# Rotary embedding on one core: tables first on the SP queue, three batch rows ahead, four tiles

## Chip, cores and metric

The kernel runs on one core of a Trainium2 chip. The metric is the device time of one execution in microseconds, as the median of several runs. The profile is one more execution, recorded by the hardware profiler.

## The reference

Each pair of neighbouring values along the last axis is rotated by an angle that depends on the position in the sequence; batch rows and heads share the tables.

```python
batch, seq_len, num_heads, head_dim = (8, 2048, 16, 64)      # x, float32
x_pairs = x.reshape(batch, seq_len, num_heads, head_dim // 2, 2)
x1 = x_pairs[..., 0]
x2 = x_pairs[..., 1]
# cos, sin: (2048, 32), broadcast over batch and heads
out1 = x1 * cos - x2 * sin
out2 = x1 * sin + x2 * cos
out = np.stack([out1, out2], axis=-1).reshape(batch, seq_len, num_heads, head_dim)
```

## The kernel before

A batch row of x is 2048 positions of 16 heads of 64 values. It is laid over 128 partitions, 16 positions each, so a row is a tile of 128 x 16384 values. In memory it is float32 (64 KB a partition); in the chip's SBUF it is bf16 (32 KB a partition). The transfers of the POOL queue, started by GpSimd, convert on the way in and on the way out.

For each batch row b, `load(b)` (L56) brings the row into a tile `xt`, `rotate` computes in place, and `store(b)` (L59) writes it out. The tiles come from a pool of `NX` = 5 buffers, so `load(5)` must wait until the store of row 0 has landed, and so on. `rotate` is three VectorE operations over the whole row: x times the sine table into a work tile `qt` (L74), x times the cosine table in place (L75), and the sum of x and `qt` with its pairs swapped (L80). The sine table `s_tab` has its second value of each pair negated, which makes the swap right.

Two pieces are handled apart. The first `HEAD` = 2 of row 0's 16 positions, the head, come as float32 over the SP queue (L84) and are cast by ScalarE into the tile (L91); `load(0, HEAD)` brings the other 14. The last `TAIL` = 4 positions of row 7, the tail, are cast by ScalarE to float32 (L118) and stored over the SP queue (L119), after a one-element copy (L117) which waits until the store of row 6 has landed. Head, `qt` and tail share one buffer of the pool `stage`.

The order is written out by hand (`tc.manual_schedule()`), and each queue takes its instructions in that order. SP: head, cosine table, sine table, and at the end the tail. POOL: the loads of rows 0 to 4, the store of row 0, a one-element copy into `mark` (L106) that reads the last loaded tile and so waits for the load of row 4, the store of row 1, and then load 5, store 2, load 6, store 3, load 7, stores 4 to 7. VectorE: the tables (L93 to L95), the head's rotation, the rest of row 0, and rows 1 to 7.

A transfer over 128 partitions is spread over the core's 16 DMA engines: 8 partitions, and so 8 packets, on each. The same 16 engines serve the SP and the POOL queue.

Of the kernel before, what the change touches and what calls it, by code (L numbers as in the profile page):

```python
# [2 lines left out]

# [4 lines left out]


@with_exitstack  # L10
def kernel(
    ctx: ExitStack,
    tc: tile.TileContext,
    x: bass.AP,
    cos: bass.AP,
    sin: bass.AP,
    out: bass.AP,
):
    nc = tc.nc
    fp32 = mybir.dt.float32  # L20
    bf16 = mybir.dt.bfloat16
    mult = mybir.AluOpType.mult
    add = mybir.AluOpType.add

    B, S, H, D = x.shape
    P = 128
    K = S // P
    KP = 16
    D2 = D // 2
    HD = H * D  # L30
    NX = 5
    HEAD = 2
    TAIL = 4


    x_t = x.rearrange("b (p k) h d -> b p k (h d)", p=P, k=K)
    out_t = out.rearrange("b (p k) h d -> b p k (h d)", p=P, k=K)
    cos_t = cos.rearrange("(p k) c -> p (k c)", p=P, k=K)
    sin_t = sin.rearrange("(p k) c -> p (k c)", p=P, k=K)

    consts = ctx.enter_context(tc.tile_pool(name="consts", bufs=1))
    xpool = ctx.enter_context(tc.tile_pool(name="xpool", bufs=NX))
    stage = ctx.enter_context(tc.tile_pool(name="stage", bufs=1))

    cos_sb = consts.tile([P, K * D2], fp32)
    sin_sb = consts.tile([P, K * D2], fp32)
    c_tab = consts.tile([P, K, D], bf16)
    s_tab = consts.tile([P, K, D], bf16)

    mark = consts.tile([1, 1], bf16)  # L50
    tiles = {}

    def load(b, k0=0):
        if b not in tiles:
            tiles[b] = xpool.tile([P, K, HD], bf16, name="xt")
        nc.gpsimd.dma_start(out=tiles[b][:, k0:], in_=x_t[b, :, k0:])  # L56

    def store(b, k1=K):
        nc.gpsimd.dma_start(out=out_t[b, :, :k1], in_=tiles[b][:, :k1])  # L59

    def rotate(b, k0, k1):
        nk = k1 - k0
        xp = tiles[b][:, k0:k1]
        qt = stage.tile([P, KP, HD], bf16, name="qt", tag="work")

        def rows(a):
            return a.rearrange("p k (h e) -> p k h e", h=H, e=D)

        def tab(a):
            return dataclasses.replace(  # L70
                a, offset=a.offset + k0 * D, ap=[a.ap[0], [D, nk], [0, H], [1, D]]
            )

        nc.vector.tensor_tensor(out=rows(qt[:, :nk]), in0=rows(xp), in1=tab(s_tab), op=mult)  # L74
        nc.vector.tensor_tensor(out=rows(xp), in0=rows(xp), in1=tab(c_tab), op=mult)  # L75
        q_swap = dataclasses.replace(
            qt, offset=qt.offset + 1, ap=[qt.ap[0], [2, nk * HD // 2], [-1, 2]]
        )
        x3 = xp.rearrange("p k (a j) -> p (k a) j", j=2)
        nc.vector.tensor_tensor(out=x3, in0=x3, in1=q_swap, op=add)  # L80

    with tc.manual_schedule():
        head = stage.tile([P, TAIL, HD], fp32, name="st", tag="work")
        nc.sync.dma_start(out=head[:, :HEAD], in_=x_t[0, :, :HEAD])  # L84
        nc.sync.dma_start(out=cos_sb, in_=cos_t)
        nc.sync.dma_start(out=sin_sb, in_=sin_t)
        load(0, HEAD)
        for b in range(1, NX):
            load(b)

        nc.scalar.copy(out=tiles[0][:, :HEAD], in_=head[:, :HEAD])  # L91
        s2 = s_tab.rearrange("p k (i j) -> p (k i) j", j=2)
        nc.vector.tensor_copy(out=s2[:, :, 0], in_=sin_sb)  # L93
        nc.vector.tensor_scalar_mul(s2[:, :, 1], sin_sb, -1.0)  # L94
        nc.vector.tensor_copy(  # L95
            out=c_tab.rearrange("p k (i j) -> p (k i) j", j=2),
            in_=cos_sb.to_broadcast([P, K * D2, 2]),
        )
        for b in range(B):
            if b == 0:  # L100
                rotate(b, 0, HEAD)
                rotate(b, HEAD, KP)
            else:
                rotate(b, 0, KP)
            if b == 1:
                nc.gpsimd.tensor_copy(out=mark, in_=tiles[NX - 1][:1, K - 1, :1])  # L106
            if b < B - 1:
                store(b)

            if b >= 1 and b - 1 + NX < B:  # L110
                load(b - 1 + NX)
        store(B - 1, K - TAIL)

        tail = stage.tile([P, TAIL, HD], fp32, name="st", tag="work")
        nc.scalar.copy(out=tiles[B - 2][:1, 0, :1], in_=tiles[B - 1][:1, K - 1, :1])  # L117
        nc.scalar.copy(out=tail, in_=tiles[B - 1][:, K - TAIL :])  # L118
        nc.sync.dma_start(out=out_t[B - 1, :, K - TAIL :], in_=tail)  # L119


# [1 line left out]
_INS = ['x', 'cos', 'sin']  # L123
_OUTS = [((8, 2048, 16, 64), 'float32')]


# [23 lines left out]
```

## Time and profile before

The median of three runs is 317.25 us (317.14 to 317.61). The profiled execution has a span of 315.5 us from the first to the last instruction.

| What | Number |
|---|---|
| Median of three runs | 317.25 us |
| Span of the profiled execution | 315.5 us |
| VectorE, a whole row, one operation (L74, L75, L80; 7 of each) | 8.69 us |
| VectorE, row 0 without its head, one operation | 7.62 us |
| VectorE, the head, one operation | 1.22 to 1.23 us |
| VectorE, three table operations L93, L94, L95 | 0.45, 0.44, 0.68 us |
| ScalarE, cast of the head (L91) and of the tail (L118) | 1.90 and 3.60 us |
| GpSimd, copy into `mark` (L106), at 102.11 us | 2.93 us |
| A transfer's issue on POOL | 0.53 to 0.67 us |
| A transfer's issue on SP | 0.35 to 0.43 us |
| Head, cosine, sine: issue to landing | 4.7, 13.4, 31.7 us |
| Load of row 0 without its head: issue to landing | 22.3 us |

The events around the queue, from the timeline in order of time (start, length, engine, line, operation, out and in, how many, and in brackets the idle time before and what ended it):

```profile
0.74 0.36 SPq L84 DMA_DIRECT2D st<-in_x_dram  x1
1.16 0.42 SPq L85 DMA_DIRECT2D cos_sb<-in_cos_dram  x1
1.24 2.80 POOL L56 DMA_DIRECT2D xt<-in_x_dram  x5 [0.80 <-PEq L145]
1.63 0.42 SPq L86 DMA_DIRECT2D sin_sb<-in_sin_dram  x1
...
61.93 0.54 POOL L59 DMA_DIRECT2D out_dram<-xt  x1 [57.89 <-DVE xt L80]
...
263.75 0.53 POOL L59 DMA_DIRECT2D out_dram<-xt  x1 [38.06 <-DVE xt L80]
295.36 0.19 ACT L117 COPY xt<-xt 1x1 bf16<-1x1 bf16 x1 [288.01 <-DMA out_dram<-xt]
295.46 3.60 ACT L118 CAST st<-xt 128x4096 f32<-128x4096 bf16 x1
299.08 0.35 SPq L119 DMA_DIRECT2D out_dram<-st  x1
```

A transfer's line shows when it was put into its queue, not when its data moved. Between the two lies the time that it stands behind earlier transfers: the store of row 0 was issued at 61.93 us, the last one at 263.75 us, 50 us before the end.

### The profile page before, as it was taken

The page shows a single profiled execution, that of the slowest core. Times are in us where ns is not written, and L with a number is a line of the kernel's source. Part 1 is how long each engine was busy: PE and PEld are TensorE (multiplying, and loading weights), DVE is VectorE, ACT ScalarE, POOL GpSimd, SP SyncE. Part 2 cuts the span into 40 slices and gives each one's busy share as a digit, 9 for nine tenths or more (in the row PEclk, how much of TensorE's full clock was granted, in tenths as well). Part 3 has the DMA queues.
Part 4 walks back from the last instruction along what each step waited for, and adds up shares of the span by engine and source line. Part 5 has one row for each costly group of instructions (what it writes and reads, how often), then busy time and mean ns, then how long its engine had stood idle before and what let it go on. Part 6 is the DMA issues. An engine that isn't in the chain of part 4 may idle for free.

```text
span 315.5 us, 125 instructions
## 1 busy us (share of the span) xinstructions
DVE 210.3 (67%) x30; ACT 6.9 (2%) x4; POOL 11.7 (4%) x21
## 2 busy tenths in 40 slices
DVE  0000799999999999999999993899509994000000
ACT  4000000000000000000000000000000000000400
POOL 3000000000000301010000100000000000000000
DMA  9899999999999999999999999999999999999997
GB/s 279 184 261 206 199 220 245 199 199 253 212 199 266 399 449 482 399 332 245 220 399 399 399 199 199 399 532 266 199 241 490 399 399 490 440 399 399 432 432 332
DMA packets 2880, 101.71 MB, mean 322 GB/s; under 512 B 320, under 2 KB 320, under 8 KB 576
## 3 DMA queue, kind: packets, MB, share of 16 engines
q0 software_dynamic: 2304, 98.04, 97.1%
q1 hardware_dynamic: 576, 3.67, 3.0%
HBM read 67.63 MB, written 67.11 MB: 427 GB/s over the span
## 4 chain that ended last, share of the span: by engine, by line
another core or an unknown queue 91%; DMA 1%; ACTq 1%; ACT 1%; issue 0%
DMA st<-in_x_dram 1%; ACTq L145 1%; ACT xt L91 1%; ACT xt L117 0%; ACTq L117 0%
## 5 line engine op out<-in xcount | busy, mean ns | idle before, releaser
L74 DVE TENSOR_TENSOR qt<-xt,s_tab 128x16384 bf16<-128x16384 bf16 (+2 forms) x9 | 69.7, 7743 | 19.1 <-DMA xt<-in_x_dram 18.8
L75 DVE TENSOR_TENSOR xt<-xt,c_tab 128x16384 bf16<-128x16384 bf16 (+2 forms) x9 | 69.7, 7743 | 0.4
L80 DVE TENSOR_TENSOR xt<-xt,qt 128x16384 bf16<-128x16384 bf16 (+2 forms) x9 | 69.7, 7744 | 0.3
L93 DVE CAST s_tab<-sin_sb 128x512 bf16<-128x512 f32 x1 | 0.5, 453 | 33.4 <-DMA sin_sb<-in_sin_dram 33.4
L59 POOL DMA_DIRECT2D out_dram<-xt x8 | 4.3, 534 | 139.9 <-DVE xt L80 139.9
L56 POOL DMA_DIRECT2D xt<-in_x_dram x8 | 4.4, 560 | 72.8 <-DMA out_dram<-xt 72.0
L117 ACT COPY xt<-xt 1x1 bf16<-1x1 bf16 x1 | 0.2, 192 | 288.0 <-DMA out_dram<-xt 288.0
L106 POOL COPY mark<-xt 1x1 bf16<-1x1 bf16 x1 | 2.9, 2929 | 39.6 <-DMA xt<-in_x_dram 39.6
L118 ACT CAST st<-xt 128x4096 f32<-128x4096 bf16 x1 | 3.6, 3598 | 0.0
L91 ACT CAST xt<-st 128x2048 bf16<-128x2048 f32 x1 | 1.9, 1897 | 3.4 <-DMA st<-in_x_dram 3.4
L91 ACT ACT_TABLE_LOAD x1 | 1.3, 1283 | 0.7 <-PEq L134 0.7
L95 DVE CAST c_tab<-cos_sb 128x1024 bf16<-128x1024 f32 x1 | 0.7, 683 | 0.0
L94 DVE TENSOR_SCALAR s_tab<-sin_sb 128x512 bf16<-128x512 f32 x1 | 0.4, 444 | 0.0
L134 POOL MEMSET const-float32-0.0<- 128x1 f32 x1 | 0.1, 100 | 0.2 <-issue 0.2
L134 POOL MEMSET const-bfloat16-1.0<- 128x1 bf16 x1 | 0.1, 102 | 0.0
L134 POOL MEMSET const-float32-1.0<- 128x1 f32 x1 | 0.1, 100 | 0.0
L134 POOL MEMSET const-uint8-127<- 128x1 uint8 x1 | 0.1, 100 | 0.0
## 6 DMA issues: line engine op xcount, KB each, us to landing
xt<-in_x_dram POOLq DMA_DIRECT2D x7, 4096.0 KB, 57.6
out_dram<-xt POOLq DMA_DIRECT2D x1, 6144.0 KB, 47.8
xt<-in_x_dram POOLq DMA_DIRECT2D x1, 3584.0 KB, 22.3
out_dram<-st SPq DMA_DIRECT2D x1, 2048.0 KB, 15.5
st<-in_x_dram SPq DMA_DIRECT2D x1, 1024.0 KB, 4.7
cos_sb<-in_cos_dram SPq DMA_DIRECT2D x1, 256.0 KB, 13.4
sin_sb<-in_sin_dram SPq DMA_DIRECT2D x1, 256.0 KB, 31.7
out_dram<-xt POOLq DMA_DIRECT2D x7, 70.1
```

Of the source, the lines that this page charges most:

```text
L56: nc.gpsimd.dma_start(out=tiles[b][:, k0:], in_=x_t[b, :, k0:])
L59: nc.gpsimd.dma_start(out=out_t[b, :, :k1], in_=tiles[b][:, :k1])
L74: nc.vector.tensor_tensor(out=rows(qt[:, :nk]), in0=rows(xp), in1=tab(s_tab), op=mult)
L75: nc.vector.tensor_tensor(out=rows(xp), in0=rows(xp), in1=tab(c_tab), op=mult)
L80: nc.vector.tensor_tensor(out=x3, in0=x3, in1=q_swap, op=add)
L91: nc.scalar.copy(out=tiles[0][:, :HEAD], in_=head[:, :HEAD])
L93: nc.vector.tensor_copy(out=s2[:, :, 0], in_=sin_sb)
L94: nc.vector.tensor_scalar_mul(s2[:, :, 1], sin_sb, -1.0)
L95: nc.vector.tensor_copy(out=c_tab.rearrange("p k (i j) -> p (k i) j", j=2), in_=cos_sb.to_broadcast([P, K * D2, 2]),)
L106: nc.gpsimd.tensor_copy(out=mark, in_=tiles[NX - 1][:1, K - 1, :1])
L118: nc.scalar.copy(out=tail, in_=tiles[B - 1][:, K - TAIL :])
L145: with _tile.TileContext(nc) as tc:
```

## The change

On SP the order becomes sine table, cosine table, head. The pool of row tiles has four buffers instead of five, and three loads instead of five are issued ahead of the first store. After that a store and a load alternate: store 0, load 3, store 1, load 4, and so on to load 7, then stores 5 to 7. The copy into `mark` is gone. ScalarE's cast of the head stands after the table operations in the text; it is on an engine of its own, so its place there changes nothing in the order of any engine. The bytes, the operations on the rows and the tail are as they were.

```diff
-    NX = 5
+    NX = 4
+    AHEAD = 3
...
-    mark = consts.tile([1, 1], bf16)
...
         head = stage.tile([P, TAIL, HD], fp32, name="st", tag="work")
+        nc.sync.dma_start(out=sin_sb, in_=sin_t)
+        nc.sync.dma_start(out=cos_sb, in_=cos_t)
         nc.sync.dma_start(out=head[:, :HEAD], in_=x_t[0, :, :HEAD])
-        nc.sync.dma_start(out=cos_sb, in_=cos_t)
-        nc.sync.dma_start(out=sin_sb, in_=sin_t)
         load(0, HEAD)
-        for b in range(1, NX):
+        for b in range(1, AHEAD):
             load(b)
-        nc.scalar.copy(out=tiles[0][:, :HEAD], in_=head[:, :HEAD])
...
+        nc.scalar.copy(out=tiles[0][:, :HEAD], in_=head[:, :HEAD])
         for b in range(B):
...
-            if b == 1:
-                nc.gpsimd.tensor_copy(out=mark, in_=tiles[NX - 1][:1, K - 1, :1])
             if b < B - 1:
                 store(b)
-
-            if b >= 1 and b - 1 + NX < B:
-                load(b - 1 + NX)
+            if b + AHEAD < B:
+                load(b + AHEAD)
         store(B - 1, K - TAIL)
```

## The prediction

> **What bounds the kernel now.** I read the page's head and its 40 slices first: who is busy at the end, and who all the time?
>
> ```profile
> span 315.5 us, 125 instructions
> DVE 210.3 (67%) x30; ACT 6.9 (2%) x4; POOL 11.7 (4%) x21
> DVE  0000799999999999999999993899509994000000
> DMA  9899999999999999999999999999999999999997
> q0 software_dynamic: 2304, 98.04, 97.1%
> HBM read 67.63 MB, written 67.11 MB: 427 GB/s over the span
> ```
>
> VectorE has a third of the span free, at both ends. The sixteen DMA engines have nothing free. Next the windows (length, then DVE, ACT and POOL busy, clock, DMA share, GB/s), one inside a load, one inside a store:
>
> ```profile
> 60.00:70.00 10.00, 9.96 (x2) 0.00 (x0) 0.54 (x1) 1.00 0.98 210
> 110.00:120.00 10.00, 9.97 (x2) 0.00 (x0) 0.00 (x0) 1.00 0.98 419
> ```
>
> GB/s counts what is written: a load reads f32 and writes bf16, so 210 there and 419 in a store are the same rate on the f32 side. Then I went to the trace's single packet records. Call Lb and Sb the load and store of batch row b (L0 without its head, S7 without its tail). Each whole transfer is eight packets on every engine, 2.43 us each in a load and 2.45 in a store, packed back to back. The first packets of the POOL queue's sixteen transfers start at:
>
> ```
> L0 5.11  L1 22.73  L2 42.25  L3 61.57  L4 80.94  S0 101.26  S1 120.57  L5 139.89
> S2 159.21  L6 178.53  S3 197.85  L7 217.17  S4 236.49  S5 255.81  S6 275.12  S7 294.44
> ```
>
> From L2 on the spacing is 19.31 to 19.32 us in either direction, except 20.32 for L4. There the last packet of every engine, at 98.0 to 98.4, took 2.99 to 3.54 us instead of 2.43: some 0.95 us that I can't explain. The tail store's packets, from 305.27, share the engines with S7's and end at 314.26. No engine pauses from its first packet (1.75 us in the earliest) to its last. So the time is 1.75 + 312.5 of packets + 1.2 to close = 315.5 us, and the median of the runs, 317.25, has 1.75 more around it.
>
> The waits show what the DMA stream hides:
>
> ```profile
> POOL xt L56 <- DMA out_dram<-xt: 72.0, 3, 37.6
> DVE s_tab L93 <- DMA sin_sb<-in_sin_dram: 33.4, 1, 33.4
> DVE qt L74 <- DMA xt<-in_x_dram: 18.8, 2, 12.4
> ```
>
> VectorE stands 33.4 us at the start for the sine table, the third transfer on SP. That looks like the thing to win, but its last operation ends at 263.5, and 51 us of stores are still queued.
>
> **The change part by part.** What can move the time is bytes, packet cost, or an engine left without a packet. The bytes stay. So each part is asked: does it leave the queue dry?
>
> *SP order.* In the records of before, once POOL's packets arrive at 5.11, each engine takes one SP packet and one POOL packet in turn; the sine table needed a turn of about 2.2 us for each of its eight packets and its completion. Now the tables' 16 packets an engine run first, at 0.084 us: 1.34 us. The head's packets are 0.309 us. Before, the earliest engine needed 2.87 us for eight of them against 2.47, so a cold start costs about 0.4. By 5.11 an engine has served (5.11 - 1.75 - 1.34 - 0.4) / 0.309 = 5 head packets. Three and the completion remain, each in a turn of 2.13 + 0.31 = 2.44: the head lands at 5.11 + 4 x 2.44 = 14.9. If POOL's packets came sooner (three issues instead of five in 2.80 us), at most all eight take turns: 5.11 + 9 x 2.44 = 27.1. The low end is 5.6, with none left.
>
> Packet cost: 144 of 256 table packets took 96 ns between POOL's instead of 84, nine an engine, 0.11 us saved. For head packets in turns the nearest rows are the tail's: 644 against 611 ns, with their neighbour at 1828 instead of 1847: +0.014 each, +0.04 for three. Sum -0.07 us; with the cold start at 0 to 0.8 instead of 0.4, -0.5 to +0.5. I take -0.1.
>
> *VectorE's start.* The head's cast (1.90) runs to 16.9, three operations of 1.23 to 20.7. L0 lands at 1.24 + 22.3 = 23.5, so the head is hidden. L0's three operations of 7.62 end at 46.5, and S0 is issued 0.6 later (as 61.36 to 61.93 before) at 47.1.
>
> *Queue order, three loads ahead, four tiles.* The queue becomes L0 L1 L2 S0 L3 S1 L4 S2 L5 S3 L6 S4 L7 S5 S6 S7: the same sixteen pieces in the same sixteen slots, since a load and a store take equally long. A whole row costs VectorE 3 x 8.73 = 26.2 us. A transfer lands about 0.45 us after its last packet, which ends 0.45 after the next slot opens; the next issue follows. Working through:
>
> ```
>       ready because                      issued   slot opens   spare
> S0    row 0 done 46.5                      47.1        61.6     14.5
> L3    fourth tile, new: no wait            47.6        80.9     33
> S1    row 1 done 72.7                      73.2       101.3     28
> L4    waits for S0 to land 81.8            81.9       120.6     39
> S2    row 2 done 98.9                      99.5       139.9     40
> L5    waits for S1 to land 121.5          121.7       159.2     37
> S3    row 3: L3 lands 102, done 128.2     128.7       178.5     50
> L6    waits for S2 to land 160            160.2       197.9     38
> S4    row 4: L4 lands 140.7, done 166.9   167.4       217.2     50
> L7    waits for S3 to land 198.7          198.9       236.5     38
> S5    row 5: L5 lands 179.3, done 205.5   206         255.8     50
> S6    row 6: L6 lands 218, done 244.2     244.7       275.1     30
> S7    row 7: L7 lands 256.6, done 282.8   283.4       294.4     11
> ```
>
> The waits of L4 to L7 have the stores S2 to S5 queued behind them on POOL. Each wait ends (81.8, 121.5, 160, 198.7) before its store's row is done (98.9, 128.2, 166.9, 205.5), so none delays a store. The copy into `mark` (2.93 us on POOL at 102.11) goes; it stood ahead of S1, due at 120.57 anyway. Nothing is saved. The tail still waits for S6 and shares with S7: unchanged.
>
> *From issue to first packet.* Only one row shows it unhidden: L0, issued at 1.24, first packet 5.11, 3.9 us, VectorE idle. An upper bound with VectorE busy is S1: issued 104.98, running at 120.57, 15.6 us, most of it surely queueing. I take 3.9, the unhidden one. S0 then has 14.5 - 3.9 = 10.6 us to spare and S7 11 - 3.9 = 7.1. With 15.6 instead, S0 would be 1.1 us late; S7's issue finds VectorE idle, so L0's row fits it.
>
> The Trainium skill speaks against this margin. "SBUF — State Buffer", Who interferes with whom, says that GpSimd can't write descriptors while VectorE runs in a mode that holds the port pair they share, and adds that two-input operations hold only the read side. The trace has a GpSimd instruction held up: the copy at L106 took 2.93 us and ended at 105.04, with VectorE's operation that ended at 105.00. It reads SBUF, so it fits the milder reading. By the severe one S0 would wait for an operation's end, at most 8.7 us, and still be in time at 55.8; by the milder one the sum stays as it is.
>
> *Sum:* 315.5 - 0.1 = 315.4; with 1.75 around it 317.2 (317.15).
>
> **Rivals.**
>
> *A. Dry before S0 (slower).* Its place is slot 61.6. If the head takes all its turns (27.1), the cast ends at 29.0, the head's operations at 32.9, L0's at 55.8, and S0 is issued at 56.4. With 3.9 it is in time at 60.3; with one VectorE operation's length, 8.69, it comes at 65.1, 3.5 us late: 320.7. It decides once issue plus preparation passes 61.6. Bounds: 1.1 late (on-time head, 15.6) to 10.4 (late head, 15.6), 318.3 to 327.6. For it: no other slot comes so early in VectorE's work. Against: two long delays must coincide. Chance 0.12.
>
> *B. A price on each turn from load to store (slower).* The 0.95 us sit exactly ahead of the first store. Before had four such turns, now six. If each paid, 5 x 0.95 more: 321.9. Against: the other three turns (at 159.21, 197.85, 236.49) show 19.32 and nothing else. Chance 0.06.
>
> *C. The 0.95 us vanish (faster).* If they belong to five loads in a row, or to S0 standing alone in the queue until 104.98, the new order drops them: 316.2. If they belong to the first write of the output, or to chance, they stay. One event can't tell. Chance 0.14.
>
> *D. VectorE's chain counts after all (faster).* Rows start at 16.9 instead of 34.66: -17.8, 299.4. Against: the full DMA row and the 51 us after VectorE's end. Chance 0.02.
>
> **How the numbers follow.** The forecast, no change, 317.2, has 0.66. A measurement of this kernel can tell some 0.2%, 0.6 us, from no change. Faster is C and D, 0.16; same 0.66; slower is A and B, 0.18. The range runs from 316.1, just under C, to 319.0, which takes in the start-up's +0.5 and A's mild end, and leaves out D, B and most of A.
>
> **What would show it.** Right: packets back to back from 1.8 to 314 us, sixteen transfers 19.32 apart; sine waited for until about 4 us instead of 33.4; head landing near 15; S0 issued near 47; VectorE waiting for loads from row 3 on; S7 issued near 283. Wrong: a gap between L2's last packet and S0's first (A); last packets of 3 us before several stores (B); none anywhere (C); or a spacing other than 19.32 in the mixed stretch, which no part of my sum allows for.

## The result, and the profile after

The changed kernel took 319.73 us in the median of six runs (317.41 to 320.98), the kernel before 317.24 (317.14 to 317.61): a ratio of 1.0068, 95% interval 1.0052 to 1.0084. It is slower by 0.7%, and its runs spread over 3.6 us where those of before spread over 0.5. The forecast of no change was wrong, and 319.73 lies above the range. (Three single runs of later variants, near 328 us, stand in the medians below and are left out of the ratios.)

The page of the changed kernel, the lines that answer to those of before:

```profile
span 317.9 us, 125 instructions
DVE  1004999999999999709993199912999039980000
DMA  7999999999999999999999999999999999999994
HBM read 67.63 MB, written 67.11 MB: 424 GB/s over the span
```

Bytes are the same and the DMA row is as full as before in its middle. The new digits are at the ends: 7 instead of 9 in the first slice, 4 instead of 7 in the last. The waits and the first and last store of rows on POOL, from its waits and its timeline:

```profile
DVE s_tab L92 <- DMA sin_sb<-in_sin_dram: 3.5, 1, 3.5
ACT xt L98 <- DMA st<-in_x_dram: 23.9, 1, 23.9
DVE qt L74 <- DMA xt<-in_x_dram: 47.6, 4, 12.5
DVE qt L74 <- ACT xt L98: 23.0, 1, 23.0
...
55.12 0.54 POOL L59 DMA_DIRECT2D out_dram<-xt  x1 [52.15 <-DVE xt L80]
...
285.56 0.53 POOL L59 DMA_DIRECT2D out_dram<-xt  x1 [38.10 <-DVE xt L80]
```

The sine table came at once, as meant, and VectorE's 33.4 us wait for it fell to 3.5. But the head, now third on SP, came at 25.9 us, and VectorE waited 23.0 us for its cast instead (ACT xt L98). The first store was still issued 6.5 us before its slot at 61.6.

So where are the 2.4 us of span? In the windows at the end (length, DVE, ACT and POOL busy, clock, DMA share, GB/s), the kernel before is silent from 314.4 us on:

```profile
314.40:315.00 0.60, 0.00 (x0) 0.00 (x0) 0.00 (x0) 1.00 0.00 0
315.00:316.00 1.00, 0.00 (x0) 0.00 (x0) 0.00 (x0) 1.00 0.00 0
316.00:316.70 0.70, 0.00 (x0) 0.00 (x0) 0.00 (x0) 1.00 0.00 0
```

The changed one isn't:

```profile
314.40:315.00 0.60, 0.00 (x0) 0.00 (x0) 0.00 (x0) 1.00 0.06 27
315.00:316.00 1.00, 0.00 (x0) 0.00 (x0) 0.00 (x0) 1.00 0.04 16
316.00:316.70 0.70, 0.00 (x0) 0.00 (x0) 0.00 (x0) 1.00 0.05 23
```

A share of 0.04 to 0.06 of sixteen engines is one engine at work. The packet records say the same. A record gives a packet's queue, start, length and size, but not its engine; which packets belong to one engine is inferred from one starting where another ends. The tail is complete on fifteen engines between 313.9 and 314.6 us, and on the sixteenth at 316.73. Every engine has an equal, fixed share of every transfer, so one that is behind can't hand its packets on; the kernel ends when it ends.

This engine can be followed back through the packet records. The others got their first POOL packet at 3.48 to 3.77 us, right behind the two tables. This one got it at 5.14: with 3.59 for the median, 1.55 us behind. In between no engine started a packet (DMA share 0.00):

```profile
3.80:5.10 1.30, 1.02 (x3) 0.00 (x0) 0.00 (x0) 1.00 0.00 0
```

Its first packet took 2.45 us instead of 2.13: 0.32 more. At the first store the last load packet of the others is some 1.2 us longer than usual; its own last two took 2.88 and 3.96 us, 1.97 more than two at 2.43: 0.75 more. 1.55 + 0.32 + 0.75 = 2.62, against 316.73 - 314.15 = 2.58 at the end. The sixteen landing times of each transfer agree: the last of them is 1.83 us behind the middle for the load of row 0, 2.58 for the load of row 2, and 2.51 to 2.59 for every whole transfer after it.

### The profile page after: what moved, and what is told of

It is laid out like the page before. It is cut to its first block, busy times and chain, and to the rows that moved or that the text cites. A ratio compares the mean times of both kernels' runs of the same rounds, so it can differ in the third digit from the quotient of the medians.

```text
span 317.9 us, 125 instructions
## 1 busy us (share of the span) xinstructions
DVE 210.5 (66%) x30; ACT 6.9 (2%) x4; POOL 8.9 (3%) x20
## 4 chain that ended last, share of the span: by engine, by line
another core or an unknown queue 85%; DMA 8%; ACTq 1%; ACT 1%; SPq 0%; issue 0%
DMA st<-in_x_dram 8%; ACTq L142 1%; ACT xt L98 1%; SPq L85 0%; SPq L84 0%; ACT xt L114 0%; ACTq L114 0%
## 5 line engine op out<-in xcount | busy, mean ns | idle before, releaser
L98 ACT CAST xt<-st 128x2048 bf16<-128x2048 f32 x1 | 1.9, 1898 | 23.9 <-DMA st<-in_x_dram 23.9
```

## The experiments

All times are medians; each kernel was timed beside runs of the kernel before on the same chip (317.61 for the first four, 317.38 for the next four, 317.64, 317.63 and 317.70 for the three pairs after that). The code shows what is changed; "..." stands for lines left out. The first four ask which part of the change does it, whether the late engine comes back, and what the lengthened packets are.

**SP's old order in the changed kernel.**

```diff
-        nc.sync.dma_start(out=sin_sb, in_=sin_t)
-        nc.sync.dma_start(out=cos_sb, in_=cos_t)
         nc.sync.dma_start(out=head[:, :HEAD], in_=x_t[0, :, :HEAD])
+        nc.sync.dma_start(out=cos_sb, in_=cos_t)
+        nc.sync.dma_start(out=sin_sb, in_=sin_t)
```

> The changed kernel with SP's old order (head, cosine, sine); three loads ahead, four tiles and the alternation stay. Theory 1 (start): in the changed kernel SP's table packets are used up by 3.7 us, the head's are not there yet, and an engine whose first POOL packet comes late (5.14 us instead of 3.5 to 3.8) stands idle and stays behind to the end; with the head first, SP's packets last beyond 5 us and cover it. It expects 317.2, spread under 0.6 us over the runs, all engines ending within 0.6 us of one another. Theory 2 (queue): the alternation of stores and loads, or the shorter batch of issues, makes one engine fall behind. It expects 319.7 as in the changed kernel, with one engine some 2 us behind the rest.

Measured: 317.34 (316.34 to 317.51), ratio 0.9987, interval 0.9979 to 0.9996. All engines ended between 314.17 and 314.33. Theory 2 falls: the queue plan alone costs nothing. No engine was late from the start: the load of row 0 landed on all sixteen between 23.15 and 23.57 us. This kernel also ran its queue dry, since with the sine last VectorE is late again. From its timeline:

```profile
61.33 8.69 DVE L74 TENSOR_TENSOR qt<-xt,s_tab 128x16384 bf16<-128x16384 bf16 x1
61.86 0.54 POOL L59 DMA_DIRECT2D out_dram<-xt  x1 [58.87 <-DVE xt L80]
```

The store was issued at 61.86, and its first packet ran at 62.97, 1.1 us later, while the VectorE operation of the first line still ran until 70.0. The engines had their last load packet through by 61.6 to 62.1, so they stood empty for 0.8 to 1.5 us. No load packet is lengthened here: the pause stands where the lengthening stood, and the store begins about when it does on fifteen engines of the changed kernel (62.97 to 63.13 here, 62.7 to 63.4 there). One of the eleven runs took 316.34, 1 us less than the rest; it has no trace.

**SP's new order alone, in the kernel before.** The two table lines go ahead of the head's as in the change; nothing else.

> The kernel before with SP's new order alone (sine, cosine, head); five loads ahead, five tiles, the copy into mark stay. Theory 1 (start): the engines run out of SP packets at 3.7 us here too, and with five issues in the first batch POOL's packets come no earlier than in the changed kernel: 318.6 to 321, spread over 1 us. Theory 2 (queue): 317.2, spread under 0.6 us.

Measured: 317.81 (317.20 to 319.78), ratio 1.0020, interval 1.0002 to 1.0037. A half miss: five of eleven runs are above 318.1, four of them above 318.6, but six show no loss. The SP order is needed for the loss, and something in the queue plan makes it frequent.

**The changed kernel again.** No edit.

> The changed kernel once more, unaltered, for a second profile and five more times. Theory 1 (start): some 319.5 with a spread of 1 to 3.5 us, and the engine that ends last is the one whose first POOL packet came last, by about the same amount plus what it loses at the first store. If instead the late engine is late from a later point (the first store, or the tail), theory 1 falls.

Measured: 319.66 (317.38 to 328.4; the 328.4 is a single run that no trace here explains). In its trace the latest first packet is at 5.49 us, 2.0 behind the median, and takes 3.02 instead of 2.13; the last engine ends at 317.09, 2.95 behind. The lateness is there at the start, as theory 1 says.

**A tiny store ahead of all others.**

```diff
         nc.sync.dma_start(out=sin_sb, in_=sin_t)
+        nc.sync.dma_start(out=out_t[0, :1, 0, :16], in_=cos_sb[:1, :16])
```

> The kernel before, with a store of 16 values of the cosine table into the first row of the output added on SP behind the three loads; the store of row 0 overwrites it. It asks what the some 0.95 us belong to by which the last load packets ahead of the first store are longer, in both kernels. If to the first write into the output, it moves to the tiny store near 15 us, and is partly hidden or not: last packets ahead of the first POOL store 2.43 us instead of 3.3, time 316.3 to 317.2. If to POOL's first turn from load to store, nothing changes: 317.2, last packets of 3.3 us at about 98 us.

Measured: 317.49 (317.34 to 317.61), ratio 0.9997, interval 0.9989 to 1.0006. The sixteen last load packets ahead of the first POOL store still took 3.01 to 3.28 us. So the lengthening does not belong to the first write into the output.

The next four ask whether it is cover that counts, whether the batch's length does, and again about the first store.

**The head second.**

```diff
         nc.sync.dma_start(out=sin_sb, in_=sin_t)
-        nc.sync.dma_start(out=cos_sb, in_=cos_t)
         nc.sync.dma_start(out=head[:, :HEAD], in_=x_t[0, :, :HEAD])
+        nc.sync.dma_start(out=cos_sb, in_=cos_t)
```

> The changed kernel with SP in the order sine, head, cosine. Theory 1 (start): what counts is that SP's packets keep every engine busy until its first POOL packet is there. Sine and head together are 0.67 + 2.47 us of packets from 1.9 us on, to about 5, with the cosine behind them: 317.2 to 317.5, spread under 0.8 us, while VectorE still gets the sine by 4 us. Rival (head's place): it is the tables being first that hurts, whatever follows, because the engines meet POOL's packets in another rhythm: 319 to 320 with a spread over 1 us.

Measured: 317.58, ten of eleven runs from 317.32 to 317.70 and one at 321.95; ratio 1.0016, interval 0.9992 to 1.0041. Sine and head, both served ahead of POOL, last to 5.3 to 5.6 us here, POOL's first packets come at 5.28 to 5.63 on all engines, and these end from 314.26 to 314.73. What counts is that SP has work for the engines until past 5 us (call it cover), not that a table is first.

**Four ahead.** `NX = 5`, `AHEAD = 4` in the changed kernel.

> The changed kernel (sine, cosine, head) with four loads ahead and five tiles, stores and loads alternating as before. The SP order alone, with five ahead, cost 0.2 to 0.6 us in the median and had 4 of 11 runs above 318.6; with three ahead it costs 2.1. If the length of the first batch of issues sets how late an engine's first POOL packet is, this lies between: 318.2 to 319.2. If it is the alternation, as 3 ahead: 319.4 to 320. If the two differ only by chance in these runs, anything from 317.5 to 319.8 with a spread over 2 us.

Measured: 319.28 (318.75 to 319.98, five runs), ratio 1.0057, interval 1.0044 to 1.0070: nearly as slow as with three, between the first two of the ranges. Four engines have their first packet at 4.11 to 4.37 us, and three end at 315.5 to 315.7.

**More cover by dummy loads.**

```diff
+    pad1 = consts.tile([P, K * D2], fp32)
+    pad2 = consts.tile([P, K * D2], fp32)
...
         nc.sync.dma_start(out=cos_sb, in_=cos_t)
+        nc.sync.dma_start(out=pad1, in_=sin_t)
+        nc.sync.dma_start(out=pad2, in_=cos_t)
         nc.sync.dma_start(out=head[:, :HEAD], in_=x_t[0, :, :HEAD])
```

> The changed kernel with both tables loaded a second time, into tiles that nobody reads, ahead of the head on SP: 16 more packets of 0.084 us on every engine, cover to about 5 us instead of 3.7. The work grows by 1.34 us. Theory 1 (start): spread under 0.8 us, engines end within 0.7 us of one another, time 317.2 + 1.3 = 318.5 at most, so faster than the changed kernel though it moves more. Rival (the late engine is late for a reason of its own, with or without packets on SP): 319.7 + 1.3 = 321, spread as in the changed kernel.

Measured: 350.52 (349.77 to 351.88), ratio 1.1046, interval 1.1024 to 1.1068. A miss for both theories, and worth the run. Only SP's first two transfers went ahead of POOL's packets. The third began at 5.70, behind each engine's first POOL packet, and from then on SP got one packet in turn with a POOL packet. Each of the two dummy loads took some 20 us in that way, and the head, fifth, landed at 66. Its timeline and its windows:

```profile
66.11 1.90 ACT L102 CAST xt<-st 128x2048 bf16<-128x2048 f32 x1 [64.09 <-DMA st<-in_x_dram]
...
95.32 0.54 POOL L61 DMA_DIRECT2D out_dram<-xt  x1 [92.34 <-DVE xt L82]
```

```profile
66.00:96.00 30.00, 27.75 (x7) 1.90 (x1) 0.68 (x2) 1.00 0.00 0
96.00:106.00 10.00, 9.97 (x2) 0.00 (x0) 0.40 (x1) 1.00 0.98 419
```

With three loads ahead POOL's queue was used up at 65.3 and SP's at 65.6; the first store was issued at 95.32, and its first packets ran at 96.43 to 96.58. For 31 us nothing moved on any engine. Those two times are the late engine's; fourteen engines were through by 63.6 and stood empty for some 33 us, about the whole loss of 33.1. This is the prediction's rival A, brought about. The pause also brought the engines into step: one was late by 1.6 us at the start (5.10), but at the end all sixteen lie between 347.64 and 347.78.

**A first store on POOL at the start, in the kernel before.**

```diff
+    z = consts.tile([16, 128], bf16)
...
         head = stage.tile([P, TAIL, HD], fp32, name="st", tag="work")
+        nc.vector.memset(z, 0.0)
+        nc.gpsimd.dma_start(out=out_t[0, :16, 0, :128], in_=z)
         nc.sync.dma_start(out=head[:, :HEAD], in_=x_t[0, :, :HEAD])
```

> The kernel before with a store of 16 x 128 zeros as the first transfer on POOL, one packet of 512 bytes an engine into a place that the store of row 0 overwrites. It asks whether the lengthening of the last load packets ahead of the first store (0.95 us) belongs to POOL's first store, since a store on SP ahead of it did not take it away. If it does, it moves to the start, where SP's packets hide it: 316.4, last packets ahead of row 0's store 2.43 us. If it belongs to the turn from a whole load to a whole store, or to the store's own issue: 317.2, 3.3 us.

Measured: 317.92 (317.46 to 318.50), ratio 1.0015, interval 1.0006 to 1.0024. The last load packets ahead of row 0's store still took 3.48 to 3.77 us. So it isn't POOL's first store as such either. It belongs to the first turn from whole loads to whole stores; why only to the first stays open.

The next four ask why one engine is late.

**The tables on ScalarE.**

```diff
-        nc.vector.tensor_copy(out=s2[:, :, 0], in_=sin_sb)
-        nc.vector.tensor_scalar_mul(s2[:, :, 1], sin_sb, -1.0)
+        nc.scalar.copy(out=s2[:, :, 0], in_=sin_sb)
+        nc.scalar.mul(s2[:, :, 1], sin_sb, -1.0)
...
+        nc.scalar.copy(out=c2[:, :, 0], in_=cos_sb)
+        nc.scalar.copy(out=c2[:, :, 1], in_=cos_sb)
```

> The changed kernel with the four table operations on ScalarE instead of the three on VectorE; VectorE does nothing before the head's rotation. It asks why one engine's first POOL packet comes late. Theory 1a (VectorE in the way): in the changed kernel VectorE's one-input table operations run from 3.5 to 4.8 us, while GpSimd still writes the first load's descriptors, and hold it up; the late engines start at 4.2 to 5.5. Without them all first packets come by 3.9 and the time is 317.2 to 317.6. Theory 1b (the spread of first packets is POOL's own): first packets as late as 4.2 to 5.5 on some engine, 319 to 320.

**The tables later.**

```diff
+    mark = consts.tile([1, 1], bf16)
...
+        nc.vector.tensor_copy(out=mark, in_=tiles[0][:1, K - 1, :1])
         nc.vector.tensor_copy(out=s2[:, :, 0], in_=sin_sb)
```

> The changed kernel with the table operations left on VectorE but held back until the load of row 0 has landed (a one-element copy ahead of them reads that tile), some 23 us instead of 3.5. The head lands at 25 us anyway, so the rows start no later than 1 us after the changed kernel's. Theory 1a (VectorE in the way): as with the tables on ScalarE, 317.2 to 317.6, first packets by 3.9. Theory 1b (POOL's own): 319 to 320, some first packets at 4.2 to 5.5. If the tables on ScalarE and the tables later differ, it is neither.

Measured: 319.72 (318.96 to 320.10, and one run at 328.46) with the tables on ScalarE, 319.21 (318.03 to 319.98, and one at 328.18) with the tables later; ratios 1.0059 (1.0046 to 1.0072) and 1.0044 (1.0030 to 1.0058). Latest first packets at 5.14 and 4.08 us, last ends at 316.63 and 316.03. With VectorE idle over the whole start one or two engines are late all the same, so VectorE is not what makes them late. The theory that the Trainium skill's rule suggests ("SBUF — State Buffer", Who interferes with whom: one-input operations of VectorE, in a mode that holds the port pair it shares with GpSimd, hold up the descriptors that GpSimd writes) does not explain this loss.

**Five issues for the same rows.**

```diff
         for b in range(1, AHEAD):
-            load(b)
+            tiles[b] = xpool.tile([P, K, HD], bf16, name="xt")
+            nc.gpsimd.dma_start(out=tiles[b][:, : K // 2], in_=x_t[b, :, : K // 2])
+            nc.gpsimd.dma_start(out=tiles[b][:, K // 2 :], in_=x_t[b, :, K // 2 :])
```

> The changed kernel with the loads of rows 1 and 2 issued in two halves each: five issues in the first batch as in the kernel before, but still three rows ahead, the same bytes, and the alternation after. SP's new order alone, with five issues, cost less (317.81, 7 of 11 runs under 317.9) than with three or four (319.3 to 319.7, 2 of 20 under 318). If the number of issues in the batch decides how often an engine's first POOL packet is late, this goes to 317.5 to 318.2 with most runs under 318. If it is what follows (three rows ahead, the alternation, the early first store): 319.2 to 320.

Measured: 317.63 (317.25 to 319.83), ratio 1.0014, interval 0.9997 to 1.0032; eight of twelve runs at 318.0 or below, the other four at 318.8 to 319.8. This is the pattern of SP's order alone, where six of eleven are under 317.9 (the expectation's seven is a miscount). So it is the first batch on POOL, not what follows it, by which the short plan makes the loss frequent.

**GpSimd waits for the sine.**

```diff
+    mark = consts.tile([1, 1], bf16)
...
+        nc.gpsimd.tensor_copy(out=mark, in_=sin_sb[:1, :1])
         load(0, HEAD)
```

> The changed kernel with a one-element copy on GpSimd ahead of the first load, which waits for the sine table: POOL issues from 3.6 us instead of 1.25, so its first packets can't come before some 5.5. It asks whether the head's packets, the third transfer on SP, would fill the engines once the tables are through at 3.7. If the head was only queued behind POOL's first packet, it runs from 3.7 to 6.2 and covers POOL's start: 317.2 to 317.8, spread under 0.8 us. If the third SP transfer is itself not there until about 5.6, all engines stand idle for 1.9 us: 319.1 or more; then the late engine on top gives 320 to 321, or, if the lateness belongs to the time 3.4 to 5.5 and not to POOL's first transfer, engines end within 0.5 us of one another.

Measured: 319.00 (318.90 to 319.35), ratio 1.0046, interval 1.0034 to 1.0058. The head ran straight behind the tables, from 3.43 us, so it had only been queued behind POOL's first packet. But it did not cover the start: while GpSimd issued, from 4.03 to 6.22 us, single packets of the head took 1.3 to 2.2 us instead of 0.31 on some of the engines, POOL's first packets began at 6.1 to 9.3 and seven took 3.0 to 4.2 instead of 2.13, and the engines ended spread from 314.6 to 316.0, the middle one at 315.0. A miss for both theories: in this kernel the slowness came while POOL's batch was issued and hit SP's packets too. With cover from the start it did not: in the kernel before, SP's old order and head second no SP packet that started between 2.7 us and POOL's first took more than 0.46.

The last pair asks what about five issues helps.

**Two tiny loads behind the three**, and **GpSimd kept at work.**

```diff
+    tiny = consts.tile([16, 2, 128], bf16)
...
         for b in range(1, AHEAD):
             load(b)
+        nc.gpsimd.dma_start(out=tiny[:, 0], in_=x_t[0, :16, 0, :128])
+        nc.gpsimd.dma_start(out=tiny[:, 1], in_=x_t[0, :16, 0, :128])
```

```diff
+    pad = consts.tile([P, 2048], fp32)
...
         for b in range(1, AHEAD):
             load(b)
+        nc.gpsimd.memset(pad, 0.0)
```

> The changed kernel with two tiny loads (16 x 128 values, one packet of 512 bytes read on each engine) issued on POOL behind the first three loads, into a tile that nobody reads: five issues, nearly the same bytes. If the number of issues in the batch decides, as with the halved rows: median 317.4 to 318.2, most runs under 318.2. If it is what the further issues bring (more packets queued early on every engine): 319 to 320, as with three.

> The changed kernel with a fill of 128 x 2048 values by GpSimd right behind the first three issues, into a tile that nobody reads, so that GpSimd is at work and not waiting until 4 us or later. If going over to the wait is what leaves one engine's first packet late: median 317.4 to 318.2. If the later issues themselves count: 319 to 320, as in the changed kernel. If GpSimd's fill holds up the writing of descriptors, later first packets and 320 or more.

Measured: 319.24 (317.39 to 320.48), ratio 1.0038, interval 1.0015 to 1.0061, and 319.38 (317.75 to 319.81), ratio 1.0048, interval 1.0030 to 1.0066. Neither heals it: it is not the count of issues alone, nor that GpSimd stops working. What sorts the eight kernels that put both tables first and issue on POOL at once (without the dummy loads, whose loss is another) is the number of packets that the first batch puts on each engine: 24, 26 or 32 (the changed kernel twice, four ahead, both table variants, the last pair) against 40 (SP's order alone, five issues). 5 of 47 runs are below 318.1, a limit drawn afterwards, with the former, 14 of 23 with the latter. That is an order, not a mechanism; why more packets help stays open.

The traces side by side, from the packet records: the start of each engine's first POOL packet, and the tail's completion on each engine.

```
                         first POOL packet     tail complete       median    traced
                         median   latest       median    last      time      run
kernel before             5.39     5.62        314.10   314.26     317.24         -
SP's old order            5.34     5.59        314.23   314.33     317.34    317.35
head second               5.41     5.63        314.50   314.73     317.58    317.70
changed kernel            3.59     5.14        314.15   316.73     319.73    319.69
changed kernel again      3.50     5.49        314.14   317.09     319.66    320.05
tables on ScalarE         3.67     5.14        314.23   316.63     319.72    319.63
two tiny loads            3.57     4.76        314.15   316.67     319.24    319.68
tables later              3.57     4.08        314.13   316.03     319.21    319.00
four ahead                3.62     4.37        314.18   315.73     319.28    318.75
SP's new order alone      3.60     4.35        314.08   314.83     317.81    317.81
five issues               3.58     3.83        314.30   315.03     317.63    318.00
GpSimd kept at work       3.45     3.77        314.20   314.74     319.38    317.75
```

The middle of the engines ends within half a microsecond in all twelve. Only the last one to three engines differ, and where POOL's first packets come at 5.3 they hardly do. The last column is the time of the run that was traced: it is 2.96 to 3.02 us above the last engine's end in all eleven rows that have it, so the last engine sets the time. The traces of the last three rows are of runs of 318.0 or less; their slower runs have no trace.

The late first packet is only part of an engine's loss. Its first packet is longer too (2.45 to 3.27 us on the engines that end over 1.5 us behind the middle, instead of 2.13), and the first turn to stores adds more. For tables later the engine is 0.51 us late at its first packet, 1.30 when the load of row 0 lands, and 1.89 from the first store on.

SP's old order was 0.1% faster than the kernel before on its chip; no variant was faster by the 0.2% that the prediction set as the least that can be told from no change.

## Why the prediction was wrong

*The bound and the slots were right.* The transfers are back to back, and the slots hold within 1.2 us on fifteen engines: L3 at 82.1 (81 forecast), S1 at 101.4 (101.3), S7 at 294.6 (294.4); S7 was issued at 285.6 (283.4).

*The step that failed* is the one on SP's order, "Packet cost", with its "-0.5 to +0.5" for the cold start. It took the sixteen engines as one. It asked what the same packets cost in sum and found nothing, which is still so for fifteen engines; but the time is that of the last engine, and that one lost 2.6 us. The row that would have told it was in the trace of before: POOL's first packets there start at 5.11 to 5.62, behind the whole head and 101 of the cosine's 128 packets. I read 5.11 as the time when POOL's packets arrive. With less SP work ahead they came at 3.4. So 5.11 was only the end of what the engines already had from SP. The prediction allowed for earlier packets where it bounded the head's landing, not where it asked what an engine does without SP's work. SP's old order and head second, with SP work until past 5 us, start evenly; that this work covers an uneven start of POOL fits them, but is inferred, since no row of before shows an uneven start. What makes one engine's start late stays open. The term "nine packets an engine at 12 ns" should have stood beside "2 us of cover goes".

*The head* landed near 25.9, not at 14.9: all eight of its packets took turns, since they started behind POOL's first packet. That was the upper end, 27.1, of the bound. It cost 8 us of VectorE's time and none of the kernel's, as the spare said.

*From issue to first packet* I took 3.9 us, with 15.6 as upper end. In the changed kernel the first load's packet came 2.2 us after its issue, so the 3.9 held SP's packets too. Two empty queues show 1.1 us with VectorE busy. The severe reading of the skill's rule on descriptors is refuted for these two-input operations: in SP's old order the packets ran 7 us before VectorE's operation ended.

*The rivals.* A had the right place, but with 6.5 us to spare it did not come about; the dummy loads on SP show it in full. Its price does not hold for a short pause: the 0.8 to 1.5 us of SP's old order, where no load packet was lengthened, cost nothing. B and C are refuted: the lengthening came once, ahead of the first store, at 59 us instead of 98, and five other turns from load to store show nothing. D is refuted: VectorE started 7 us earlier, and nothing came of it. The side that happened, slower, had 0.18, and not by its mechanism: none of the rivals was about one engine.

## What to carry to other kernels

Where DMA bounds a kernel and each engine has a fixed share of every transfer, the time is that of the engine that falls behind; read the end and the start of the packet records engine by engine, not the mean busy share. Before a short transfer is moved out of a queue's start because "nothing waits for it", ask what it keeps busy there: here, with 2.5 us of a plain load near the front of one queue, the other queue started evenly on all engines, and without it it often did not. And a third transfer on SP is not early merely because it is issued at 1.6 us.

## What the runs showed of the hardware

- In the changed kernel the late engine stayed 2.51 to 2.59 us behind from 63 to 295 us. A pause of the queue levels the engines: with the dummy loads one was 2.2 us behind before 31 us of empty queue, and they ended within 0.15 us of one another; in SP's old order some 1.2 us brought a spread of 0.5 down to 0.16.
- With both tables first, SP's two transfers ran ahead of POOL's first packet on each engine and the third behind it, though it was issued at 1.63 us; in the kernel before the head and 101 of the cosine's 128 packets ran ahead. From then on the two queues alternate packet by packet. "DMA: Bandwidth & Descriptors", Queues, rings and completion order, in the Trainium skill lets an engine drain a packet of typically some 9 to 17 descriptors before it turns to another queue. Here the turn is shorter, one row: a row of 2 KB on SP alternates with a row of 28 KB (as written) on POOL, so that a dummy load's eight rows took some 20 us.
- Where GpSimd waited for the sine, single packets of the head took 1.3 to 2.2 us instead of 0.31 while POOL's first batch was issued; in the kernel before, with POOL issuing from 1.24 us, no SP packet between 2.7 us and POOL's first took more than 0.44.
- GpSimd's fill of 128 x 2048 values held up VectorE. From the timeline of the kernel with GpSimd kept at work:

```profile
2.95 1.84 POOL L91 MEMSET pad<- 128x2048 f32 x1
3.53 1.57 DVE L94 CAST s_tab<-sin_sb 128x512 bf16<-128x512 f32 x1 [3.53 <-DMA sin_sb<-in_sin_dram]
```

The cast takes 0.45 us elsewhere; here it ended at 5.10, 0.3 us after the fill. This fits the Trainium skill ("SBUF — State Buffer", Who interferes with whom): a cast of VectorE can take a mode that needs the port pair shared with GpSimd, and whichever of the two starts first blocks the other.
